# A mixer's triangular solve laid out one 16x16 block a partition, its row loads and decays grouped, a full-width matmul, and an output norm on a chain of its own

## The chip, the cores and the metric

The kernel runs on one core of one Trainium2 chip. The metric is the device time of one execution in microseconds (us), as the median of several runs. A core has five engines that run side by side, each through its own queue of instructions in order: TensorE (PE; its weight loads are shown as PEld), VectorE (DVE), ScalarE (ACT), GpSimd (POOL) and SyncE (SP). SyncE computes nothing here; it issues every transfer between the chip's memory and the core's on-chip memory (SBUF). TensorE writes into PSUM, eight banks of accumulators. On-chip memory has 128 partitions.

## The reference

One decoder layer over 256 tokens of width 2048, in float32: a SwiGLU feed-forward block, a token mixer, a second feed-forward block, and a last norm. Each of the three blocks is preceded by a norm that is shifted and scaled by a conditioning vector, and its result is gated by that vector. The change lies in the mixer:

```python
proj = h @ w_in                      # q, k, v of both head groups, gates, z
# heads 0..7 "fox": softmax attention with a decay given by summed log-sigmoid gates, then a norm
# heads 0..7 "gdn": gated delta rule over chunks of 64 tokens
decay = exp(where(incl, g[..., :, None] - g[..., None, :], -inf))
lower = where(strict, einsum("bhnid,bhnjd->bhnij", kb, k) * decay, 0.0)
t_inv = triangular_solve(eye + lower, eye)          # 64 x 64, unit lower triangular
u = t_inv @ vb;  w = t_inv @ (kb * exp(g))
a_intra = where(incl, einsum("bhnid,bhnjd->bhnij", q, k) * decay, 0.0)
# for each chunk: v_new = u - w @ state;  o = (q * exp(g)) @ state + a @ v_new;  state is updated
o_g = rmsnorm(o_g) * silu(z)
return concatenate([o_f, o_g]) @ w_out
```

So each gdn head needs, for each of its four chunks, the inverse of a 64 x 64 unit lower triangular matrix, and then a chain through four chunks.

## The kernel before

**Weights.** All weight matrices are cut into tiles of 128 x 128 and packed in the order of use. `Stream.next` loads eight tiles at a time (512 KB, `wraw`, L92), ScalarE rounds the block (`whi`, L95) and VectorE takes the rest (`wlo`, L98), so that products of two or three passes reach float32 accuracy. Three buffers of each kind let loads run ahead. Between the blocks the modulation columns are computed at a rate given by `RATE`: a load of 1 MB (`adat`, L212) and a product with a sum on VectorE (L214).

**Order of the work.** The program is written out by Python loops. Projections of the mixer are written by `project` (weights stationary, L613 to L615) and `project_rows` (activations stationary, L626 to L628). After each weight tile `tick` adds 0.35 us to a counter, and when a chain's due time has come, the next piece of that chain is written at this place: a chain is a Python generator, and `yield 1.4` says that its next piece is due 1.4 us later (times a factor `GAP`). Each kind of chain ("k" for keys and solve, "gdn", "fox") runs its members one after the other. `finish` writes what is left of a chain at once. The build then orders each engine's queue starting from this order and its own estimate of what is ready, and sets all waits; the queue's order on the chip is fixed, so an instruction that waits holds all behind it on its engine. `tc.issue_after(x)` keeps an instruction behind x in its queue.

**The sequence.** `ORDER` is a list of steps: K (keys of one gdn head), G (its queries and values), F (a fox head), Z and V (gates z and fox values of four heads). The first projection takes the gates and K0 to K2 together. Then follow K3 to K7, Z0, G0, V0, F0, G1 and so on, and last the out projection of 256 tiles, four output columns first.

**Gates, keys, solve.** `gates` computes running sums of the gates, writes them as rows to DRAM (`rows`, L700) and keeps columns in `colS`. `keys(h)` loads a head's row, broadcast to all partitions (`row_of`, L712), makes the decay from it (`decay(h, 0)`, L723 and L725), and leaves `Ln[:, h]` = -beta k k^T decay (L770). After four heads `solve` inverts the 16 x 16 diagonal blocks of these four heads' two tiles of 128 x 128: 8 tiles with 8 blocks each. It stores the blocks to DRAM (`ld`, eight transfers, L783) and reads them back so that each of a block's 16 partitions holds the whole block (eight broadcast reads of 128 KB, L788), into columns of `x`, which the mixer uses as spare room: `x` itself is kept in `xd` in DRAM meanwhile and comes back by `x_back` (L600). Then 15 steps of a product (L795) and a sum (L796) on VectorE substitute, and L798 spreads the result into `U0`. `gdn(h)` starts with `U0` (L818, L820) and doubles the block size twice, 16 to 32 to 64.

**The chunk loop** of `gdn` (L899 to L921): `wq` holds, per tile, the four slots of 64 columns w, q, q, w. One matmul (L908) gives both w times state and q times state in two halves of a PSUM bank; L909 makes the new values in `vz`, whose other half is zero; L911 adds a times the new values to the half that holds q times state; L915 gives the state's update. Then `orw` is normed and gated (L924 to L933), and after `yield 7.0` it is transposed (L938) and split for the out projection.

**The end.** After the last step all chains are finished, `x_back` is called for all four quarters, and the out projection runs over its operands in the order `ko`: gdn 0 to 3, fox 0 to 7, gdn 4 to 7.

Of the kernel before, what the change touches and what calls it, by code (L numbers as in the profile page):

```python
# [16 lines left out]
P = 128  # L17
# [24 lines left out]
GAP = {"k": 1.0, "gdn": 1.0, "fox": 1.2}  # L42
ORDER = ("K3 K4 K5 K6 K7 Z0 G0 V0 F0 G1 F1 G2 F2 G3 F3 V1 Z1 G4 F4 G5 F5 G6 F6 G7 F7").split()
# [6 lines left out]
for _k, _w in (  # L50
    ("foxm", 384), ("mL", 128), ("mU", 128), ("zm", 2 * 64), ("blk", 4), ("id16", 16),
    ("tri", 128), ("tri64", 128), ("tru64", 128), ("sgn", GR),
):
    CST[_k] = (_n, _w)
    _n += _w
# [54 lines left out]
def layer_kernel(ctx: ExitStack, tc: tile.TileContext, xt, c, adaw, cols, cst, w, out, order, dbg=None):  # L110
# [222 lines left out]
    chains = {"k": [], "gdn": [], "fox": []}  # L333
    due = {"k": 0.0, "gdn": 0.0, "fox": 0.0}
# [240 lines left out]
    def mixer():  # L575
# [5 lines left out]
        ld = dram("ld", [2 * NH, 8, 16, 16])  # L581
# [61 lines left out]
        def gates(ps):  # L643
# [61 lines left out]
            V.tensor_scalar(ng, colS[:, :, 1], -1.0, None, ALU.mult)  # L705
            yield 1.0

        def row_of(h, kind, tag):

            rb = m2p.tile([P, T], F32, name="rw", tag="rw" + tag)  # L710
            with tc.issue_after(W.last):
                nc.sync.dma_start(rb, rows[h : h + 1, kind * T : (kind + 1) * T].broadcast_to([P, T]))  # L712
            return rb
# [4 lines left out]
        def decay(h, up):  # L718

            gb = row_of(h, 1, "g")  # L720
            gbv = gb.rearrange("p (t j) -> p t j", t=2)
            dd = m2p.tile([P, 2, P], F32, name="dec", tag=f"dec{up}")
            V.tensor_tensor(dd, bc(C("mU" if up else "mL")), gbv, ALU.add if up else ALU.subtract)  # L723
            for t in range(2):
                A.activation(dd[:, t], dd[:, t], AF.Exp, bias=ng[:, t, h : h + 1] if up else colS[:, t, 1, h : h + 1])  # L725
            if up:
                A.activation(gb, gb, AF.Exp)
            return dd, gb

# [17 lines left out]
        def keys(h):  # L747
# [3 lines left out]
            dec, _ = decay(h, 0)  # L751
            yield 1.0
# [16 lines left out]
            for t in range(2):  # L769
                V.scalar_tensor_tensor(Ln[:, h, t], pg[:, t * P : (t + 1) * P], nb2[:, t : t + 1], dec[:, t], ALU.mult, ALU.mult)  # L770

        def solve(half):
# [7 lines left out]
            Lh = Ln[:, hs4].rearrange("p h t j -> p (h t) j")  # L780
            for b in range(8):
                r = slice(16 * b, 16 * b + 16)
                nc.sync.dma_start(ld[ht, b].rearrange("n r c -> r n c"), Lh[r, :, r])  # L783
            rows_ = x[:, ht]
            for b in range(8):
                r = slice(16 * b, 16 * b + 16)
                src = ld[ht, b].rearrange("n r c -> n (r c)").unsqueeze(0).to_broadcast([16, n, 256])
                nc.sync.dma_start(rows_[r], src)  # L788
            yield 9.0
            U = tmp.tile([P, n, 16], F32, name="u16", bufs=1)  # L790
            pr = tmp.tile([P, n, 16], F32, name="pr16", bufs=1)
            G.memset(rows_[:, :, 0:256:17], 1.0)
            V.tensor_copy(U, C("id16").unsqueeze(1).to_broadcast([P, n, 16]))
            for i in range(1, 16):
                V.tensor_tensor(pr[:, :, : i + 1], rows_[:, :, 16 * i : 16 * i + i + 1], U[:, :, : i + 1], ALU.mult)  # L795
                V.tensor_reduce(U[:, :, i], pr[:, :, : i + 1], mybir.AxisListType.X, ALU.add)  # L796
            for q in range(2):
# [3 lines left out]
                    C("blk").unsqueeze(1).unsqueeze(3).to_broadcast([P, 4, 4, 16]), ALU.mult)  # L801
            yield 1.0
# [3 lines left out]
        def gdn(h):  # L806
# [59 lines left out]
            V.tensor_tensor(wq[:, :, 1:3, :], q_[:, 0].rearrange("p (t c i) -> p t c i", t=2, c=2),  # L866
# [25 lines left out]
            V.tensor_copy(wq[:, :, 0:4:3, :], pu[:, T:].rearrange("p (t c i) -> p t c i", t=2, c=2))  # L892
# [5 lines left out]
            for c_ in range(4):  # L898
# [7 lines left out]
                else:  # L906
                    new = vz[:, c_ - 1]
                    PE.matmul(pc_, wq[:, t, 2 * ev : 2 * ev + 2].rearrange("p a i -> p (a i)"), st, start=True, stop=True)  # L908
                    V.tensor_sub(new[r], u[r, t], pc_[r])  # L909
# [290 lines left out]
```

## Time and profile before

| what | value |
|---|---|
| time, median of 3 runs | 2102.22 us (2100.92 to 2103.65) |
| the profiled execution's own time | 2100.31 us |
| its span, first to last instruction | 2098.5 us |
| TensorE busy | 2041.5 us (97%) |
| VectorE busy | 1565.8 us (75%) |
| ScalarE busy | 1013.5 us (48%) |
| mean TensorE clock granted | 0.982 |
| read from HBM | 514.74 MB |

In the lists of the profile a group of instructions is shown as line, engine, operation, output <- inputs, shapes, xcount, then busy us, the mean ns of one, and idle time of the engine before them with what ended it. A list of waits reads: who waited <- for whom: us in total, times, longest. SPq and DVEq are the engines' queues. A timeline gives start, length, engine, line, operation and names. A list of transfers gives count, KB each, and the median us from issue to landing. A stretch's PE clock is the share of full speed that was granted.

### The profile page before, as it was taken

Reading aid. Unit: us, or ns where it says so; the run is one execution under the profiler, and the core shown is the slowest. Engines: PE = TensorE matmul, PEld = TensorE weight load, DVE = VectorE, ACT = ScalarE, POOL = GpSimd, SP = SyncE. Lnnn points to the kernel's source line nnn. Section 1 sums busy time; section 2 is a strip of 40 time slices with the busy share of each in tenths; the row PEclk is TensorE's granted clock in tenths of the full one; section 3 lists DMA queues with packets and bytes.
Section 4 is the critical chain, followed back from the end, with each engine's and each line's share of the span. In section 5 each row is a group of like instructions: output and inputs, shape, how many; then the busy total and the mean of one; then the engine's idle time right before and its main releaser. Section 6 shows DMA issues by size and latency. Waiting matters only on the chain.

```text
span 2098.5 us, 33387 instructions
## 1 busy us (share of the span) xinstructions
PE 2041.5 (97%) x12965; PEld 1828.9 (87%) x12966; DVE 1565.8 (75%) x2394; ACT 1013.5 (48%) x1579; POOL 63.7 (3%) x58
## 2 busy tenths in 40 slices
PE   8999999999999999889999999999999999999997
PEld 6999999888888888779989978788888888888886
DVE  6899878888888988877878878866666555555554
ACT  4544544333444446645656644554443344444442
POOL 0000000000000120000000002000000000000011
PEclk8999999999999999999999999999999999999998
DMA  8989867999888885765666567566766555555553
GB/s 313 349 324 324 278 206 265 358 344 362 331 327 334 326 292 176 209 249 215 229 231 221 212 210 284 206 239 224 240 234 217 188 184 190 184 188 190 185 188 111
DMA packets 129488, 521.26 MB, mean 248 GB/s; under 512 B 16425, under 2 KB 21545, under 8 KB 111153
## 3 DMA queue, kind: packets, MB, share of 16 engines
q1 hardware_dynamic: 129330, 519.13, 70.1%
q8 instruction: 102, 1.67, 0.3%
q14 instruction: 56, 0.46, 0.1%
HBM read 514.74 MB, written 4.34 MB: 247 GB/s over the span
## 4 chain that ended last, share of the span: by engine, by line
PE 90%; DVE 5%; DMA 2%; ACT 1%; issue 1%; SPq 0%; DVEq 0%; ACTq 0%; POOL 0%; POOLq 0%
PE pd L361 15%; PE pu L361 11%; PE pg L361 11%; PE pd L362 8%; PE pg L362 5%; PE pu L362 5%; PE pgu L431 5%; PE pgu L429 5%; PE pgu L430 5%; PE pp L613 3%; PE pp L614 3%; PE pp L615 3%; PE po L361 3%; DVE wlo L98 2%; PE po L362 1%; DMA wraw<-in_w_dram 1%
## 5 line engine op out<-in xcount | busy, mean ns | idle before, releaser
L98 DVE TENSOR_TENSOR wlo<-wraw,whi 128x1024 fp32r<-128x1024 f32 x674 | 824.2, 1229 | 347.7 <-ACT whi L95 344.4
L95 ACT CAST whi<-wraw 128x1024 fp32r<-128x1024 f32 x674 | 701.4, 1047 | 681.8 <-issue 172.3
L361 PE MATMUL pd<-hid,whi 128*128 128x512 f32 x1408 | 497.2, 397 | 0.0
L362 PE MATMUL pd<-hid,wlo 128*128 128x256 f32 x1408 | 396.1, 282 | 0.8 <-DVE wlo L98 0.7
L361 PE MATMUL pg<-hs,whi 128*128 128x512 f32 x960 | 342.1, 397 | 2.3 <-DVE hs L304 1.8
L361 PE MATMUL pu<-hs,whi 128*128 128x512 f32 x960 | 342.9, 398 | 0.0
L214 DVE CUSTOM_DVE_ANT_0 adat<-adat,cs,colt 128x2048 f32<-128x2048 f32 x140 | 329.2, 2352 | 14.2 <-DMA adat<-in_ada_dram 13.8
L361 PEld LDWEIGHTS pd<-hid,whi 128*128 128x128 f32 x1408 | 264.2, 188 | 64.8
L362 PE MATMUL pg<-hs,wlo 128*128 128x256 f32 x960 | 270.4, 282 | 0.0
L362 PE MATMUL pu<-hs,wlo 128*128 128x256 f32 x960 | 269.9, 281 | 0.0
L362 PEld LDWEIGHTS pd<-hid,wlo 128*128 128x128 f32 x1408 | 265.5, 189 | 2.5 <-DVE wlo L98 2.1
L429 PE MATMUL pgu<-hs,whi 128*128 128x256 f32 x896 | 251.2, 283 | 4.6 <-ACT hs L300 3.8
L431 PE MATMUL pgu<-hs,wlo 128*128 128x256 f32 x896 | 250.8, 284 | 2.4 <-DVE wlo L98 2.3
L430 PE MATMUL pgu<-hs,whi 128*128 128x256 f32 x896 | 252.4, 283 | 0.0
L361 PEld LDWEIGHTS pg<-hs,whi 128*128 128x128 f32 x960 | 180.7, 188 | 45.7 <-issue 2.1
L361 PEld LDWEIGHTS pu<-hs,whi 128*128 128x128 f32 x960 | 180.7, 188 | 43.9
L613 PE MATMUL pp<-hs,whi 128*128 128x256 f32 x656 | 192.8, 295 | 6.7 <-ACT whi L95 5.3
L615 PE MATMUL pp<-hs,wlo 128*128 128x256 f32 x656 | 188.4, 288 | 1.6 <-DVE wlo L98 1.6
L614 PE MATMUL pp<-hs,whi 128*128 128x256 f32 x656 | 188.6, 287 | 0.0
L362 PEld LDWEIGHTS pg<-hs,wlo 128*128 128x128 f32 x960 | 181.7, 189 | 0.0
L362 PEld LDWEIGHTS pu<-hs,wlo 128*128 128x128 f32 x960 | 181.6, 189 | 0.0
L429 PEld LDWEIGHTS pgu<-hs,whi 128*128 128x128 f32 x896 | 170.8, 191 | 6.0 <-ACT hs L300 4.2
(306 smaller groups left out, 2436.6 us busy)
## 6 DMA issues: line engine op xcount, KB each, us to landing
wraw<-in_w_dram SPq DMA_DIRECT2D x674, 512.0 KB, 4.2
adat<-in_ada_dram SPq DMA_DIRECT2D x140, 1024.0 KB, 6.6
rw<-rowd SPq DMA_DIRECT2D x24, 128.0 KB, 6.6
x<-in_x_dram SPq DMA_DIRECT2D x4, 512.0 KB, 5.8
adaf<-in_ada_dram SPq DMA_DIRECT2D x4, 512.0 KB, 8.0
adaf<-in_ada_dram SPq DMA_DIRECT2D x2, 1024.0 KB, 11.8
xd<-x SPq DMA_DIRECT2D x4, 512.0 KB, 6.4
x<-ld SPq DMA_DIRECT2D x16, 128.0 KB, 6.1
```

Source lines behind the costliest of these rows:

```text
L95: nc.scalar.copy(self.h, r)
L98: nc.vector.tensor_tensor(self.l, r, self.h.bitcast(F32), ALU.subtract)
L214: V.tensor_tensor_reduce(t, t, cs, 1.0, L("adab", q, 1), ALU.mult, ALU.add, mod[:, q : q + 1])
L361: PE.matmul(ps, wt[0], act.rearrange("p a t -> p (a t)"), start=first, stop=False)
L362: PE.matmul(ps[:, :T], wt[1], act[:, 0], start=False, stop=last)
L429: PE.matmul(o, wh, hs[:, k, 0], start=first and s == 0, stop=False, skip_group_check=skip)
L430: PE.matmul(o, wh, hs[:, k, 1], start=False, stop=False, skip_group_check=skip)
L431: PE.matmul(o, wl, hs[:, k, 0], start=False, stop=last, skip_group_check=skip)
L613: PE.matmul(pp[i][:, :T], wh, hs[:, k, 0], start=(k == 0), stop=False)
L614: PE.matmul(pp[i][:, :T], wh, hs[:, k, 1], start=False, stop=False)
L615: PE.matmul(pp[i][:, :T], wl, hs[:, k, 0], start=False, stop=(k == KD - 1))
```

## The change

The blocks of `L` now go to one partition each: 64 partitions hold 64 blocks of 16 x 16. The eight stores to DRAM stay, two at a time with yields between them; one read brings the 64 blocks back; the substitution runs with products of i x i elements in step i (rows of the inverse kept transposed); the result is stored (`lt`), and read back in the layout of `U` in pieces of 16 numbers. Every one of these transfers is kept behind the weight load written last.

The keys' decays are made for four heads at once, in `Ln` itself: one transfer (`fetch_rows`) brings four rows to `x`'s columns, one subtraction and eight exponentials make them (`decays`), and `keys` multiplies in place. The second half's rows are fetched after the first half's solve. `decay(h)` is left for queries only, and its row, like the fox heads' rows, is now requested before the head's projection.

In the chunk loop `wq` holds q, w, w, q, so that L908's q half lies where the chunk's own rows lie, and L911 uses all 128 columns of `At` and writes the whole bank. The output's transposes become a chain "out" of their own. G7 is put before F6. The chains are no longer finished before the out projection: they go on between its tiles, each is finished where its operand is first used, and `x_back` is called before the first group's last operand. `V1` first finishes the "k" chain.

```diff
-GAP = {"k": 1.0, "gdn": 1.0, "fox": 1.2}
-ORDER = ("K3 K4 K5 K6 K7 Z0 G0 V0 F0 G1 F1 G2 F2 G3 F3 V1 Z1 G4 F4 G5 F5 G6 F6 G7 F7").split()
+GAP = {"k": 1.0, "gdn": 1.0, "fox": 1.2, "out": 1.0}
+ORDER = ("K3 K4 K5 K6 K7 Z0 G0 V0 F0 G1 F1 G2 F2 G3 F3 V1 Z1 G4 F4 G5 F5 G6 G7 F6 F7").split()
...
-        ld = dram("ld", [2 * NH, 8, 16, 16])
+        ld = dram("ld", [2 * NH, 8, 256])
+        lt = dram("lt", [2 * NH, 8, 256])
...
+            yield 2.0
+            fetch_rows(0)
             yield 1.0
 
         def row_of(h, kind, tag):
 
-            rb = m2p.tile([P, T], F32, name="rw", tag="rw" + tag)
+            rb = m2p.tile([P, T], F32, name="rw", tag="rw" + tag, bufs=3 if tag == "g" else 2)
...
-        def decay(h, up):
-
-            gb = row_of(h, 1, "g")
+        def decay(h):
+
+            gb = rowg.pop(h)
...
+        def fetch_rows(half):
+
+            rowk[half] = x[:, 4 * half : 4 * half + 4]
+            src = rows[4 * half : 4 * half + 4, T:]
+            with tc.issue_after(W.last):
+                nc.sync.dma_start(rowk[half], src.unsqueeze(0).to_broadcast([P, 4, T]))
+
+        def decays(half):
+
+            hs4 = slice(4 * half, 4 * half + 4)
+            yield 5.0
+            rv = rowk[half].rearrange("p h (t j) -> p (h t) j", t=2)
+            mL = C("mL").unsqueeze(1).to_broadcast([P, 8, P])
+            V.tensor_tensor(Ln[:, hs4].rearrange("p h t j -> p (h t) j"), mL, rv, ALU.subtract)
+            for h in range(4 * half, 4 * half + 4):
+                for t in range(2):
+                    A.activation(Ln[:, h, t], Ln[:, h, t], AF.Exp, bias=colS[:, t, 1, h : h + 1])
+            yield 1.0
...
-            dec, _ = decay(h, 0)
-            yield 1.0
...
-                V.scalar_tensor_tensor(Ln[:, h, t], pg[:, t * P : (t + 1) * P], nb2[:, t : t + 1], dec[:, t], ALU.mult, ALU.mult)
+                V.scalar_tensor_tensor(Ln[:, h, t], pg[:, t * P : (t + 1) * P], nb2[:, t : t + 1], Ln[:, h, t], ALU.mult, ALU.mult)
...
+            yield 1.5
             for b in range(8):
                 r = slice(16 * b, 16 * b + 16)
-                nc.sync.dma_start(ld[ht, b].rearrange("n r c -> r n c"), Lh[r, :, r])
-            rows_ = x[:, ht]
-            for b in range(8):
-                r = slice(16 * b, 16 * b + 16)
-                src = ld[ht, b].rearrange("n r c -> n (r c)").unsqueeze(0).to_broadcast([16, n, 256])
-                nc.sync.dma_start(rows_[r], src)
-            yield 9.0
-            U = tmp.tile([P, n, 16], F32, name="u16", bufs=1)
-            pr = tmp.tile([P, n, 16], F32, name="pr16", bufs=1)
-            G.memset(rows_[:, :, 0:256:17], 1.0)
-            V.tensor_copy(U, C("id16").unsqueeze(1).to_broadcast([P, n, 16]))
+                with tc.issue_after(W.last):
+                    nc.sync.dma_start(ld[ht, b].rearrange("n (r c) -> r n c", r=16), Lh[r, :, r])
+                if b % 2:
+                    yield 1.4
+            yield 2.0
+            B = slice(0, 8 * n)
+            blk, xt_, pr = (x[B, j] for j in range(4, 7))
+            with tc.issue_after(W.last):
+                nc.sync.dma_start(blk, ld[ht].rearrange("n b e -> (n b) e"))
+            yield 6.0
+            G.memset(xt_, 0.0)
+            G.memset(xt_[:, 0:256:17], 1.0)
+            bv, xv, pv = (t_.rearrange("p (i j) -> p i j", i=16) for t_ in (blk, xt_, pr))
             for i in range(1, 16):
-                V.tensor_tensor(pr[:, :, : i + 1], rows_[:, :, 16 * i : 16 * i + i + 1], U[:, :, : i + 1], ALU.mult)
-                V.tensor_reduce(U[:, :, i], pr[:, :, : i + 1], mybir.AxisListType.X, ALU.add)
+                V.tensor_tensor(pv[:, :i, :i], xv[:, :i, :i], bv[:, i, :i].unsqueeze(1).to_broadcast([8 * n, i, i]), ALU.mult)
+                V.tensor_reduce(xv[:, :i, i], pv[:, :i, :i], mybir.AxisListType.X, ALU.add)
+            yield 5.0
+            with tc.issue_after(W.last):
+                nc.sync.dma_start(lt[ht].rearrange("n b e -> (n b) e"), xt_)
+            yield 3.0
+            U = x[:, 7, :P].rearrange("p (n i) -> p n i", n=n)
+            with tc.issue_after(W.last):
+                nc.sync.dma_start(U, lt[ht].rearrange("n b (q i) -> (b q) n i", q=16))
+            yield 5.0
...
+            if half == 0:
+                fetch_rows(1)
             yield 1.0
...
-            V.tensor_tensor(wq[:, :, 1:3, :], q_[:, 0].rearrange("p (t c i) -> p t c i", t=2, c=2),
+            V.tensor_tensor(wq[:, :, 0:4:3, :], q_[:, 0].rearrange("p (t c i) -> p t c i", t=2, c=2),
...
-            V.tensor_copy(wq[:, :, 0:4:3, :], pu[:, T:].rearrange("p (t c i) -> p t c i", t=2, c=2))
+            V.tensor_copy(wq[:, :, 1:3, :], pu[:, T:].rearrange("p (t c i) -> p t c i", t=2, c=2))
...
-                    V.tensor_sub(new[r], u[r, t], pc_[r])
+                    V.tensor_sub(new[r], u[r, t], pc_[ro])
                     yield 1.2
-                PE.matmul(pc_[ro], At[:, t, 64 * ev : 64 * ev + 64], new, start=(c_ == 0), stop=True,
-                          skip_group_check=True)
+                PE.matmul(pc_, At[:, t], new, start=(c_ == 0), stop=True, skip_group_check=True)
...
-            A.copy(orw[:64], pov[64:, :, 0])
-            A.copy(orw[64:], pov[:64, :, 1])
+            A.copy(orw[:64], pov[:64, :, 0])
+            A.copy(orw[64:], pov[64:, :, 1])
...
-            yield 7.0
+            start("out", h, to_out(h, orw))
+            yield 0.2
+
+        def to_out(h, orw):
+            yield 6.0
             pt_ = pss("pot")
...
-            cb = row_of(h, 0, "f")
+            cb = rowf.pop(h)
...
+            if h % 4 == 0:
+                start("k", h, decays(h // 4))
             start("k", h, keys(h))
...
+                rowg[h] = row_of(h, 1, "g")
...
+                finish("out", h - 3)
...
-                ups[h] = decay(h, 1)
+                ups[h] = decay(h)
...
+                if h:
+                    finish("k", NH)
                 pv = project_rows("vf", h)
...
+                rowf[h] = row_of(h, 0, "f")
...
-        for kind in chains:
-            finish(kind, NH)
-        for q in range(4):
-            x_back(q)
-
-
-        ko = [NH + h for h in range(4)] + list(range(NH)) + [NH + h for h in range(4, NH)]
+
+
+        ko = [NH + h for h in range(4)] + list(range(6)) + [NH + h for h in range(4, NH)] + [6, 7]
...
             for i, k in enumerate(ko):
+                for kind in ("gdn", "out") if k >= NH else ("fox",):
+                    finish(kind, k % NH)
+                if js[0] == 0 and i == KD - 1:
+                    for q in range(4):
+                        x_back(q)
                 for q, j in enumerate(js):
                     mm(pj[q], W.next("o", k, j), oh_[k], i == 0, i == KD - 1)
+                    tick(TILE_US)
```

More of the change, by code (lines that the diff above doesn't have):

```diff
@@ L50 @@
 for _k, _w in (
-    ("foxm", 384), ("mL", 128), ("mU", 128), ("zm", 2 * 64), ("blk", 4), ("id16", 16),
+    ("foxm", 384), ("mL", 128), ("mU", 128), ("zm", 2 * 64), ("blk", 4),
     ("tri", 128), ("tri64", 128), ("tru64", 128), ("sgn", GR),
@@ L332, in layer_kernel @@
     clock = {"now": 0.0}
-    chains = {"k": [], "gdn": [], "fox": []}
-    due = {"k": 0.0, "gdn": 0.0, "fox": 0.0}
+    chains = {"k": [], "gdn": [], "fox": [], "out": []}
+    due = {k: 0.0 for k in chains}
     def advance(kind):
@@ L716, in mixer @@
         bh = lambda c_, n: c_.unsqueeze(1).to_broadcast([n, 2, 64])
-        def decay(h, up):
-            gb = row_of(h, 1, "g")
+        def decay(h):
+            gb = rowg.pop(h)
             gbv = gb.rearrange("p (t j) -> p t j", t=2)
-            dd = m2p.tile([P, 2, P], F32, name="dec", tag=f"dec{up}")
-            V.tensor_tensor(dd, bc(C("mU" if up else "mL")), gbv, ALU.add if up else ALU.subtract)
+            dd = m2p.tile([P, 2, P], F32, name="dec")
+            V.tensor_tensor(dd, bc(C("mU")), gbv, ALU.add)
             for t in range(2):
-                A.activation(dd[:, t], dd[:, t], AF.Exp, bias=ng[:, t, h : h + 1] if up else colS[:, t, 1, h : h + 1])
-            if up:
-                A.activation(gb, gb, AF.Exp)
+                A.activation(dd[:, t], dd[:, t], AF.Exp, bias=ng[:, t, h : h + 1])
+            A.activation(gb, gb, AF.Exp)
             return dd, gb
+        rowg, rowf, rowk = {}, {}, {}
+        def fetch_rows(half):
[13 more added lines that the diff above has]
+            yield 1.0
         Tms = [m1p.tile([P, 2, P], F32, name=f"Tm{i}") for i in range(2)]
@@ L1108, in constants @@
     put("blk", ic // 16 == np.arange(4)[None, :])
-    put("id16", i % 16 == np.arange(16)[None, :])
     put("tri", i <= j)
```

## The prediction

> **What bounds the kernel now.** I read the page first, then 10 us windows, then TensorE's waits, then SyncE's own timeline.
>
> ```profile
> span 2098.5 us, 33387 instructions
> PE 2041.5 (97%) x12965; PEld 1828.9 (87%) x12966; DVE 1565.8 (75%) x2394; ACT 1013.5 (48%) x1579; POOL 63.7 (3%) x58
> ```
>
> TensorE sets the time, so a change pays only where TensorE stands, runs at a lower clock, or does something dearly. The mixer runs from about 794 to 1331 us. Two places in it stand out.
>
> ```profile
> 860.00:920.00 60.00, 45.36 (x237) 38.60 (x236) 46.80 (x135) 28.18 (x57) 0.62 (x2) 0.83 0.78 212
> 1230.00:1250.00 20.00, 14.85 (x72) 11.37 (x71) 11.10 (x36) 7.59 (x18) 0.00 (x0) 0.74 0.43 134
> 860.00:870.00 10.00, 8.58 (x49) 7.04 (x47) 8.07 (x32) 6.32 (x26) 0.00 (x0) 1.00 0.82 110
> ```
>
> Columns: stretch, length, busy PE, PEld, DVE, ACT, POOL, then PE clock, DMA share, GB/s. From 860 to 920 PE is idle 60 - 45.36 = 14.6 us, and the clock averages 0.83, so 0.17 x 60 = 10.2 us of clock is missing. Clock missing while PE stands costs nothing more; I count 6 of the 10.2 as falling on work (two waits, below, lie partly in the slow time). Lost there: about 21 us. From 1230 to 1250 it is 5.15 idle and 0.26 x 20 = 5.2 of clock, again about half on work: about 8 us.
>
> ```profile
> PE pv L626 <- ACT whi L95: 5.9, 1, 5.9
> PE pp L613 <- ACT whi L95: 5.3, 1, 5.3
> PE pp L615 <- DVE wlo L98: 1.6, 1, 1.6
> ```
>
> In the first place PE waits for weights. SyncE's timeline (start, length, line, count) says why:
>
> ```profile
> 850.47 1.82 SPq L92 DMA_DIRECT2D wraw<-in_w_dram  x2
> 852.34 0.42 SPq L212 DMA_DIRECT2D adat<-in_ada_dram  x1
> 853.33 1.08 SPq L712 DMA_DIRECT2D rw<-rowd  x2
> 857.15 4.14 SPq L783 DMA_DIRECT2D ld<-Ln  x8
> 861.33 3.75 SPq L788 DMA_DIRECT2D x<-ld  x8
> 865.48 0.34 SPq L712 DMA_DIRECT2D rw<-rowd  x1
> 866.20 1.32 SPq L92 DMA_DIRECT2D wraw<-in_w_dram  x2
> ```
>
> No weight block is issued from 852.3 to 866.2, 13.9 us, because solve's sixteen transfers and the row loads stand in the queue. Behind them the eight broadcast reads move 1 MB at 110 GB/s with the DMA engines 82% busy (window 860 to 870). The cover can be read here: a hold of 13.9 us cost PE a 5.9 us wait, so about 7 to 8 us without a weight issue is hidden. The second half does the same:
>
> ```profile
> 879.33 3.89 SPq L783 DMA_DIRECT2D ld<-Ln  x8
> 883.32 3.69 SPq L788 DMA_DIRECT2D x<-ld  x8
> 887.10 11.68 SPq L92 DMA_DIRECT2D wraw<-in_w_dram  x4
> ```
>
> The second place is the end of the mixer: head 7's chain has no projection left to hide under, and the out projection waits for its last operands.
>
> **Part 1: solve and rows.** Per half the change keeps the eight stores, replaces the eight broadcast reads with one read of 64 KB, and adds a store and a read of 64 KB after the substitution.
>
> ```profile
> rw<-rowd SPq DMA_DIRECT2D x24, 128.0 KB, 6.6
> x<-ld SPq DMA_DIRECT2D x16, 128.0 KB, 6.1
> ld<-Ln SPq DMA_DIRECT2D x16, 8.0 KB, 2.7
> ```
>
> (Last number: us from issue to landing.) Issues per half: 16 become 11, and not in one row: the stores go two at a time between weight blocks. The eight row loads for the keys become two of 512 KB. The broadcast megabyte goes. Three dependencies are new: the read waits for the stores (2.7 us by the row above), the last read waits for the store before it (at most 6.1, the row of a larger transfer), and that store waits for VectorE. All but the last lie under the 7 us of cover, so I cost them at nothing; if the cover is gone each costs its own length. The other moved DMAs (a gdn head's row load and a fox head's, now ahead of their projections) pass weight blocks in the queue with one issue each, 0.34 to 0.54 us; nothing is late behind them.
>
> How a read in 64-byte pieces goes is not in the trace. The stores, 128 pieces of 64 bytes, land in 2.7 us; the eight reads, 1024 pieces of 1 KB, occupied the DMA for about 8 us. The read of U has 1024 pieces of 64 bytes, so its cost lies between these; I take 3 us, nearer the stores because the pieces have their size. The Trainium skill (DMA: Bandwidth & Descriptors, Specifications) asks for at least 512 bytes a transfer and says that below it the engine does read-modify-write. If by that rule U's read were as dear as the reads that it replaces, half 0 would keep 8 us and the sum would give 2080 (a rival, below); the stores of 64 bytes here show no such price.
>
> VectorE's work in the stretch, and how it moves:
>
> ```profile
> L795 DVE TENSOR_TENSOR pr<-x,u 128x16 f32<-128x16 f32 (+14 forms) x30 | 7.0, 232 | 4.5 <-DMA wraw<-in_w_dram 2.5 <-POOL x L792 1.4
> L796 DVE TENSOR_REDUCE u<-pr 128x8 f32<-128x16 f32 (+14 forms) x30 | 6.8, 227 | 0.7
> L770 DVE SCALAR_TENSOR_TENSOR Ln<-pkk,nb,dec 128x128 f32<-128x128 f32 x16 | 5.0, 346 | 0.2
> 850.00:911.80 61.80, 47.93 (x262) 41.57 (x261) 49.95 (x155) 31.59 (x69) 0.62 (x2) 0.83 0.78 211
> 911.80:966.00 54.20, 53.43 (x348) 46.92 (x347) 41.53 (x73) 32.00 (x61) 0.00 (x0) 1.00 0.65 238
> ```
>
> The substitution is (7.0 + 6.8)/2 = 6.9 us a half. In the new layout instruction i has i x i elements a partition in place of 8(i+1): 1240 against 1080 in all.
>
> ```profile
> 872.44 0.17 DVE L795 TENSOR_TENSOR pr<-x,u 128x16 f32<-128x16 f32 x1 [1.36 <-POOL x L792]
> 888.33 0.29 DVE L795 TENSOR_TENSOR pr<-x,u 128x128 f32<-128x128 f32 x1
> ```
>
> 112 more elements cost 0.12 us, 1.1 ns each, so 160 more, in two instructions, cost 0.35 us a half: nothing. These rows also show that 6.9 us of work took 16 us, because weights (L98), modulation (L214) and the other half's keys stood between.
>
> Going by the yields and 0.35 us a weight tile, the old program writes the second half's substitution 76 us after the mixer's first matmul, inside G0. The new one writes it at 110 us, in F0, after keys 4 to 7 at 87 to 93 us; U0 of half 0 comes at 77, before head 0 wants it at 87. So about 6.9 + 0.8 + 2.5 + 1.3 = 11.5 us of VectorE work (substitution, U0, half of L770, its small companions) leaves a stretch where VectorE was busy 49.95 of 61.8 us, and lands in one with 54.2 - 41.5 = 12.7 us free. Nearly all of that stretch's slack is then used, and wlo, which PE waits for, is on the same engine. **I give back 4 us for it, and 2 us for head 0 arriving at U0 early**; between nothing and all 21 regained I take 15.
>
> **Part 2: At at full width.** The attention matmul of the state loop (L911) used 64 columns; it becomes 128. Rows: start, length.
>
> ```profile
> 984.22 0.28 PE L615 MATMUL pp<-hs,wlo 128*128 128x256 f32 x1
> 984.34 0.38 PE L908 MATMUL po<-st,wq 128*128 128x128 f32 x2
> 984.47 0.36 PE L613 MATMUL pp<-hs,whi 128*128 128x256 f32 x1
> 984.67 0.28 PE L614 MATMUL pp<-hs,whi 128*128 128x256 f32 x1
> ```
>
> From L615 to L614 is 0.45 us with two wide matmuls of 0.12 in it, so the two passes of the 128-column L908 cost 0.21.
>
> ```profile
> 995.35 0.28 PE L615 MATMUL pp<-hs,wlo 128*128 128x256 f32 x1
> 995.56 0.43 PE L911 MATMUL po<-vz,At 128*64 128x128 f32 x2
> 995.92 0.39 PE L613 MATMUL pp<-hs,whi 128*128 128x256 f32 x1
> 996.15 0.28 PE L614 MATMUL pp<-hs,whi 128*128 128x256 f32 x1
> ```
>
> Here the same sum is 0.80 - 0.24 = 0.56: the narrow pair costs 0.34 more. There are 8 heads x 4 = 32 of them: 10.9 us, on the engine that bounds, in stretches where PE is busy throughout. The nearest row for the new form is L908: same bank, same shape. From below the gain is nothing (the price is of something else, or VectorE then bounds); I take 9.5, since VectorE, 41.5 of 54.2 us busy in the stretch quoted and fuller with the moved work, may hold back a little. The swapped halves of wq only rename rows; the copies and the subtraction keep their shapes and cost the same.
>
> **Part 3: the end.** The out norm's transposes become a chain of their own, so head h+1 starts 7 us of yields earlier; G7 goes before F6; the closing steps are written between the out projection's tiles instead of before them. By the yields, head 7's output is then ready 9 us after F7 and first used 18 us after it. So the 8 us should go. Against that x_back, 2 MB, moves to the end of the first group.
>
> ```profile
> 1219.60:1261.00 41.40, 36.25 (x204) 30.15 (x204) 25.75 (x66) 17.26 (x37) 0.00 (x0) 0.88 0.63 220
> SPq L600 <- DVE orw L933: 9.5, 1, 9.5
> x<-xd SPq DMA_DIRECT2D x4, 512.0 KB, 4.5
> ```
>
> Today SyncE stands 9.5 us at x_back for head 7, weights behind it, while PE stands anyway. Moved, it no longer waits, but PE no longer stands either: its price is between nothing (512 KB land in 4.5 us, and 7 us are covered) and 6 us (2 MB at 220/0.63 = 349 GB/s, this stretch's rate with the DMA engines full). I take 2: gain 6. One pool of three PSUM banks now serves the out chain and the next head together: nothing, because the transposes come 6 us apart, and up to 2 us in all if each head waits 0.3.
>
> **The sum.** 15 + 9.5 + 6 = 30.5 us. The profiled execution took 2100.3 us (span 2098.5 and 1.8 around it), 1.9 under the median of the runs. 2100.3 - 30.5 = 2069.8, on the median's footing 2071.7: **2071 us**.
>
> **Rivals.**
> - **Head 0 stands at U0** (16%). The new route to U0 has three DMA round trips and a substitution that took 16 us for 6.9 of work; PE takes its queue in order. For it: by the yields there are only 10 us between U0 and its use. Against it: DMA is freed there. One wait like today's 5.9, with 3 of clock, would take 9 of the 15: 2081. The Trainium skill (TensorE: Matmul & The Clock Gate, Why this matters for your kernels) puts the loss of the clock at gaps above some 3 us; by that a wait under 3 costs only itself, 2075 at most; the two waits above, both longer, do show the low clock.
> - **U's small pieces are dear** (4%): its 1024 pieces occupy the DMA engines as the 1024 of the old reads did, 8 us in which weights wait; half 1's lie far from any use. 2080. Against it: the 2.7 us of the stores.
> - **The narrow price stays or VectorE takes it** (12%): no 9.5, so 2081. For it: VectorE's fill in the stretches after 911. Against: L908 beside it.
> - **x_back takes what the end gains** (8%): 6 us of weights late in place of 2, so 2076.
> - **Slower: SyncE is held by the new dependent transfers** (7%). Seven waits (read, store, read in each half, and the second row load behind U0) each hold the queue longer than the 7 us covered. The second hold today (879.3 to 887.1) cost PE 5.3 us, 1.6 for a late wlo, and some 2.7 of clock, 9.6; seven make 67, against 40 gained: 2129. It decides from five of the seven. For it: VectorE needed 16 us where the yields leave 6. Against: SyncE's waits for such results are short today, since the queue's order puts weights ahead:
>
> ```profile
> SPq L783 <- DVE pr L795: 1.8, 1, 1.8
> ```
>
> - **The parts cancel** (5%): the four before the slower one together give back 9 + 8 + 9.5 + 4 = 30.5, so 2102.
>
> **How the numbers follow.** Forecast 48%, its own range 2062 (all 40 us regained) to 2078; rivals in their order 16, 4, 12, 8, 7 and 5%. The range 2058 to 2090 leaves out the slower case and the cancelled one; below 2062 it allows for small waits elsewhere in the mixer. A measurement of this kernel tells about 0.2%, 4.2 us, from no change: faster 0.88 (48 + 16 + 4 + 12 + 8), same 0.05, slower 0.07.
>
> **What would show it.** In the new profile: no weight gap over 8 us on SyncE between 850 and 920 us, and no slow clock there (Part 1); L911's successors at the same spacing as L908's, 0.21 us a pair (Part 2); no PE wait for orw and a first out group of about 64 x 0.35 = 22 us plus chain work, where it took 41 (Part 3). It is wrong if PE waits for U0 in pu0 or for wlo for over 6 us in V0 to G1, if weights wait behind lt or x_back, or if the second PE gap only moves.

## The result: a third less than forecast

The changed kernel takes **2081.4 us** (median of 4 runs, 2078.4 to 2086.5) where the kernel before, in the same session, takes 2102.0 (2100.9 to 2103.7): a ratio of 0.9905, 95% interval 0.9893 to 0.9918. That is 20.6 us less; 30.5 were forecast, with 2071 us as the time. The page's first lines:

```profile
span 2076.6 us, 33353 instructions
PE 2029.3 (98%) x12965; PEld 1825.4 (88%) x12966; DVE 1559.8 (75%) x2386; ACT 1012.5 (49%) x1577; POOL 66.8 (3%) x60
```

The span fell by 21.9 us (the profiled execution was the shortest of its four). To see where, I cut both traces where the last projection matmul of each step (for the out groups, the last of each group) starts. The rows below are, in order, Z0, G0, all from V0 to F7, the first group of the out projection (four columns, 64 tiles), and its second (one column, 16 tiles). Columns as in the prediction: length, busy PE, PEld, DVE, ACT, POOL, clock, DMA share, GB/s. Before:

```profile
854.38:889.84 35.46, 28.43 (x122) 22.62 (x121) 29.81 (x100) 18.61 (x46) 0.31 (x1) 0.86 0.81 200
889.84:911.72 21.88, 15.04 (x104) 14.49 (x103) 15.81 (x45) 8.53 (x12) 0.31 (x1) 0.77 0.76 234
911.72:1219.55 307.83, 306.94 (x2233) 282.55 (x2232) 247.51 (x543) 189.43 (x394) 0.00 (x0) 1.00 0.62 223
1219.55:1261.12 41.57, 36.42 (x206) 30.27 (x204) 25.92 (x66) 17.26 (x37) 0.00 (x0) 0.88 0.64 221
1261.12:1267.34 6.22, 5.83 (x33) 4.83 (x32) 6.22 (x10) 3.56 (x6) 3.94 (x3) 1.00 0.72 267
```

After:

```profile
855.50:879.31 23.81, 22.96 (x104) 18.42 (x103) 20.16 (x56) 12.02 (x25) 0.00 (x0) 1.00 0.68 242
879.31:893.53 14.22, 12.46 (x97) 11.79 (x96) 11.86 (x20) 11.19 (x14) 0.00 (x0) 1.00 0.74 242
893.53:1209.29 315.76, 311.50 (x2312) 292.22 (x2310) 262.04 (x625) 194.94 (x423) 0.43 (x2) 1.00 0.64 224
1209.29:1234.88 25.59, 25.43 (x151) 21.92 (x150) 18.66 (x46) 12.56 (x27) 0.00 (x0) 1.00 0.78 284
1234.88:1243.70 8.82, 6.42 (x33) 4.89 (x32) 6.51 (x11) 4.98 (x8) 5.18 (x3) 1.00 0.49 192
```

| stretch | before | after | difference |
|---|---|---|---|
| Z0 and G0 | 57.3 | 38.0 | -19.3 |
| V0 to F7 | 307.8 | 315.8 | +7.9 |
| out, first group | 41.6 | 25.6 | -16.0 |
| out, second group | 6.2 | 8.8 | +2.6 |

Both bad places are gone: the clock is 1.00 in all five rows, where it was 0.86, 0.77 and 0.88. But PE's idle time between V0 and F7 went from 0.9 us (307.83 - 306.94) to 4.3, 79 more matmuls lie there, and the second out group now has 2.4 us of idle time. The time before Z0 (1.1 us more) and after the second out group (1.7 more) make up the rest of the difference in span.

### The profile page after: what moved, and what is told of

The parts are those of the page before. It is cut to its first block, busy times and chain, and to the rows that moved or that the text cites. A ratio compares the mean times of both kernels' runs of the same rounds, so it can differ in the third digit from the quotient of the medians.

```text
span 2076.6 us, 33353 instructions
## 1 busy us (share of the span) xinstructions
PE 2029.3 (98%) x12965; PEld 1825.4 (88%) x12966; DVE 1559.8 (75%) x2386; ACT 1012.5 (49%) x1577; POOL 66.8 (3%) x60
## 4 chain that ended last, share of the span: by engine, by line
PE 87%; DVE 6%; DMA 2%; ACT 2%; issue 1%; DVEq 0%; SPq 0%; ACTq 0%
PE pd L361 15%; PE pu L361 11%; PE pg L361 11%; PE pd L362 8%; PE pg L362 5%; PE pu L362 5%; PE pgu L431 5%; PE pgu L429 5%; PE pgu L430 5%; PE po L361 3%; PE pp L614 2%; PE pp L616 2%; PE pp L615 2%; DVE wlo L98 2%; PE po L362 1%
## 5 line engine op out<-in xcount | busy, mean ns | idle before, releaser
L214 DVE CUSTOM_DVE_ANT_0 adat<-adat,cs,colt 128x2048 f32<-128x2048 f32 x140 | 329.3, 2352 | 16.5 <-DMA adat<-in_ada_dram 16.1
```

The source lines that it names most:

```text
L214: V.tensor_tensor_reduce(t, t, cs, 1.0, L("adab", q, 1), ALU.mult, ALU.add, mod[:, q : q + 1])
```

## What the signs say that the prediction named

SyncE's timeline of the changed kernel (start, length, line, count), around the first half's stores:

```profile
852.52 0.33 SPq L92 DMA_DIRECT2D wraw<-in_w_dram  x1
852.90 0.43 SPq L212 DMA_DIRECT2D adat<-in_ada_dram  x1
858.15 4.66 SPq L806 DMA_DIRECT2D ld<-Ln  x8
862.91 0.86 SPq L92 DMA_DIRECT2D wraw<-in_w_dram  x2
863.99 0.52 SPq L813 DMA_DIRECT2D x<-ld  x1
```

Between 850 and 920 there is one gap without a weight block over 8 us, from 852.9 to 862.9: the eight stores were issued together after all, in spite of the yields between them. PE lost little by it: it was idle for 23.81 - 22.96 = 0.85 us in all of Z0. So here 10 us without a weight load were nearly covered, where the prediction read 7 to 8. It isn't a fixed number: before the change the second hold left 10.0 us without a weight load too (877.1 to 887.1), and PE stood 5.3 us for it. The difference may be that weights were already late there from the first hold; no run tests it. No wait of PE for U0 exists. One sign of being wrong did come true: weights wait behind `x_back`, and PE stands 2.4 us for them in the second out group (see the run with the loads apart). The reads of the new route land in about 5 us, where the prediction took 3 for U's (count, KB, us from issue to landing):

```profile
x<-ld SPq DMA_DIRECT2D x2, 64.0 KB, 4.8
x<-lt SPq DMA_DIRECT2D x2, 64.0 KB, 5.4
```

U's read (`x<-lt`) in 1024 pieces of 64 bytes takes 5.4 us, the read of as many bytes in 64 pieces of 1 KB 4.8. The Trainium skill (DMA: Bandwidth & Descriptors, Specifications) asks for 512 bytes or more in a transfer for the full rate. At this size the trace shows 0.6 us more for the smaller pieces (medians of two reads each, at different times), not the 8 us by which the prediction's rival priced it.

For the full-width matmul, two places of PE's timeline (start, modelled length). Before, a narrow pair L911 with the state's update L915 behind it:

```profile
982.24 0.28 PE L614 MATMUL pp<-hs,whi 128*128 128x256 f32 x1
982.45 0.43 PE L911 MATMUL po<-uz,At 128*64 128x128 f32 x2
982.81 0.49 PE L915 MATMUL pst<-uz,kbd 128*128 128x128 f32 x2
983.06 0.36 PE L615 MATMUL pp<-hs,wlo 128*128 128x256 f32 x1
983.26 0.28 PE L613 MATMUL pp<-hs,whi 128*128 128x256 f32 x1
```

After, such two pairs (L945, L948) where nothing stands between:

```profile
972.48 0.28 PE L615 MATMUL pp<-hs,whi 128*128 128x256 f32 x1
972.60 0.38 PE L945 MATMUL po<-vz,At 128*128 128x128 f32 x2
972.82 0.39 PE L948 MATMUL pst<-vz,kbd 128*128 128x128 f32 x2
972.96 0.36 PE L616 MATMUL pp<-hs,wlo 128*128 128x256 f32 x1
973.16 0.28 PE L614 MATMUL pp<-hs,whi 128*128 128x256 f32 x1
```

With 0.12 taken off for each of the two wide matmuls, as in the prediction, the two pairs cost 1.02 - 0.24 = 0.78 us before and 0.68 - 0.24 = 0.44 after: the full 0.34. Where two such pairs stand alone between projection matmuls (worked out from the starts in the traces), the median went from 0.78 at 19 places to 0.49 at 20 (the expectation below took 0.53). Half of the 20 lie at 0.44 to 0.46; at the others, up to 0.74, a pair starts late.

## The experiments

Each time stands against the kernel before, run beside it; "gain" is the difference of the medians.

### One part at a time

**At alone**: the kernel before with only this.

```diff
-            V.tensor_tensor(wq[:, :, 1:3, :], ...q...)
+            V.tensor_tensor(wq[:, :, 0:4:3, :], ...q...)
...
-                PE.matmul(pc_[ro], At[:, t, 64 * ev : 64 * ev + 64], new, ...)
+                PE.matmul(pc_, At[:, t], new, start=(c_ == 0), stop=True, skip_group_check=True)
...  (the other half of wq, the subtraction and the copies of orw follow)
```

> The kernel before with Part 2 alone: L911 at 128 columns, the halves of wq swapped. Theory of the prediction: a narrow pair costs 0.34 us more than a wide one, 32 pairs, so 9.5 to 10.9 us, about 2092. From the changed kernel's trace, where the wide pair with its successor still takes 0.53 us in place of 0.44, I would now say 7 to 9: 2093 to 2095. Rival (the price is not the width's, or VectorE takes it): within 4 us of 2102.

Measured: 2098.6 us, ratio 0.9988 (0.9978 to 0.9997), a gain of 2.2.

**The end alone**: the chain "out", G7 before F6, closing steps between the out projection's tiles, `x_back` in the first group.

```diff
...
+            start("out", h, to_out(h, orw))
...
-        for kind in chains:
-            finish(kind, NH)
-        for q in range(4):
-            x_back(q)
...
+                if js[0] == 0 and i == KD - 1:
+                    for q in range(4):
+                        x_back(q)
```

> The kernel before with Part 3 alone: the out chain, G7 before F6, the closing steps between the out projection's tiles, x_back before the last operand. Prediction: 6 us, 2096. Rival (x_back takes what the end gains): 2100 to 2102, with PE waiting for whi or wlo behind x_back in the second group of the out projection for more than 5 us. In the changed kernel that wait is 2.4 us in all, so I lean to 2097.

Measured: 2097.7, ratio 0.9984 (0.9975 to 0.9994), a gain of 3.1.

**Solve and rows alone**: the changed kernel with the other two parts undone.

> The changed kernel without Parts 2 and 3, that is, the kernel before with the new solve, the grouped decays and the row loads ahead. Prediction: 15 us, 2087. If the three parts simply add (21 us in all, 8 for Part 2, 5 for Part 3), 8 us: 2094. If the clean stretch of the changed kernel (Z0 and G0 take 38.0 us there, 57.3 before) holds here too and nothing is given back later, 18: 2084.

Measured: 2089.6, ratio 0.9946 (0.9929 to 0.9963), a gain of 11.2.

**The changed kernel with the narrow At** (the first diff reversed).

> The changed kernel with L911 narrow again, Parts 1 and 3 kept. If Part 2 is worth the same here as alone, the time is that of the changed kernel plus the gain of Part 2 alone: 2081 + 8 = 2089 (prediction's size: 2091). If VectorE bounds the stretches after G0 in the changed kernel, where more of its work lies, the narrow price is partly hidden: 2082 to 2085.

Measured: 2086.7, ratio 0.993 (0.9915 to 0.9944), a gain of 14.1, so that At is worth about 6 us there (20.6 - 14.1 = 6.5 by the gains, 2086.7 - 2081.4 = 5.3 by the times), where alone it was worth 2.2. In its trace the stretch from G0's end to F7's end is 7.7 us longer than the changed kernel's, and all of that is PE's busy time (319.3 against 311.5). The second out group is 2.7 us longer there as well (11.5 against 8.8), where no narrow matmul runs, so the 5 to 6 us aren't purely At's. The three solo gains add to 16.5, the whole gives 20.6: the parts seem to help each other. The rows from G0's end to F7's end say how. At alone, then the end alone (with its second out group), then both in the kernel before:

```profile
912.24:1217.93 305.69, 300.72 (x2234) 283.09 (x2232) 246.45 (x538) 189.11 (x394) 0.00 (x0) 1.00 0.63 224
```

```profile
911.52:1227.10 315.58, 314.53 (x2286) 288.87 (x2284) 251.12 (x558) 192.20 (x403) 0.00 (x0) 1.00 0.62 220
1253.57:1263.91 10.34, 7.92 (x34) 6.16 (x32) 7.11 (x11) 4.42 (x7) 5.17 (x3) 0.83 0.53 211
```

```profile
911.47:1220.72 309.25, 308.08 (x2285) 289.35 (x2284) 249.66 (x558) 194.35 (x405) 0.00 (x0) 1.00 0.63 225
```

**At and the end together**, without the new solve:

> The kernel before with Part 2 (At at full width) and Part 3 (the end), without the new solve. Alone the two gave 2.2 and 3.1 us. If their gains are independent, together they give 5.3: some 2095. If Part 2's saving was eaten in the kernel before because G0 to F7 waits on each head's chain, and the out norm as a chain of its own starts the next head earlier and so takes these waits away, the two together give 9 to 12: 2089 to 2092. If they get in each other's way, under 4: over 2097.

Measured: 2091.6, ratio 0.995 (0.9936 to 0.9965), a gain of 9.2, which is more than 2.2 + 3.1 and at the lower edge of the second theory. At alone takes 6.2 us of busy time from PE (306.94 to 300.72), but PE's idle time rises from 0.9 to 5.0 us. My reading is that PE, which takes its queue in order, now reaches a matmul before VectorE or ScalarE has its operand, and that the narrow pairs' extra time had covered that. Its waits there are short, the longest two by the list of waits (the first is for a weight block's low part, the second for an operand of a gdn chain):

```profile
PE pp L615 <- DVE wlo L98: 1.3, 1, 1.3
PE pn L860 <- DVE Z L837: 1.1, 1, 1.1
```

With the out norm on a chain of its own the same saving (314.53 to 308.08, 6.5) leaves PE's idle time as it is (1.05 and 1.17), and the stretch is 6.3 us shorter. So Part 2's gain hangs on Part 3; which of Part 3's edits does it was not separated. And 9.2 + 11.2 = 20.4: these two groups add up to the whole.

### The solve: queue or megabyte

**The old solve, its transfers written two at a time between weight blocks.**

```diff
-                nc.sync.dma_start(ld[ht, b].rearrange("n r c -> r n c"), Lh[r, :, r])
+                with tc.issue_after(W.last):
+                    nc.sync.dma_start(ld[ht, b].rearrange("n r c -> r n c"), Lh[r, :, r])
+                if b % 2:
+                    yield 1.4
...  (the eight reads likewise)
-            yield 9.0
+            yield 5.0
```

> The kernel before with solve's own transfers spread: the eight stores and the eight broadcast reads of 128 KB are kept, but go two at a time between weight blocks, with 1.4 us between the pairs. If the loss in the first stretch came from SyncE standing at sixteen transfers in a row, most of what the new solve gains alone (11 us) comes back: 2091 to 2094. If it came from the broadcast megabyte, which keeps the DMA engines full for 8 us at 110 GB/s, the weights stay late: 2098 to 2102.

Measured: 2115.1, ratio 1.0073 (1.0058 to 1.0088): 15 us slower. Z0 and G0 take 33.09 + 13.41 = 46.5 us, 10.8 less than before, but V0 goes from 29.9 to 54.9:

```profile
904.05:958.92 54.87, 39.02 (x156) 30.34 (x155) 33.03 (x82) 18.52 (x36) 0.31 (x1) 0.75 0.49 155
```

On SyncE the transfers of the first half still went out in one row, eight stores and eight reads, with no weight block between 859.9 and 870.8:

```profile
860.33 5.63 SPq L784 DMA_DIRECT2D ld<-Ln  x8
866.00 3.75 SPq L792 DMA_DIRECT2D x<-ld  x8
```

Of the second half's only the reads were parted, four and four. The edit did delay the work: the second half's substitution moved into V0, where head 0's chain wants VectorE and ScalarE (PE waits 4.0 us for a transpose's operand behind a product of the substitution, 3.7 for `At`; ScalarE 8.9 for PE). So this edit didn't spread the transfers as it was meant to, and the run doesn't tell the queue from the megabyte.

**The old solve with short reads**: all sixteen transfers stay, each read brings one row of a block, 8 KB for 128 KB. The rest of each block is zero, so what is inverted is not L.

```diff
+            if h in (0, 1):
+                G.memset(x[:, 8 * h : 8 * h + 8], 0.0)
...
-                src = ld[ht, b].rearrange("n r c -> n (r c)").unsqueeze(0).to_broadcast([16, n, 256])
-                nc.sync.dma_start(rows_[r], src)
+                src = ld[ht, b, 0].unsqueeze(0).to_broadcast([16, n, 16])
+                nc.sync.dma_start(rows_[r, :, :16], src)
```

> The kernel before, whose eight broadcast reads a half read only the first row of each block (8 KB a transfer where it was 128 KB; the rest of the blocks is set to zero by GpSimd once, so the inverse computed is not that of L). The number of transfers and their place in SyncE's queue stay. If the loss between Z0 and the end of G0 (57 us, of which 38 after the change) comes from SyncE's queue being held, as the prediction's reading of the cover has it, Z0 and G0 stay at 55 to 58 us and the time within 2 us of before. If it comes from the megabyte that the reads move while weights want the same DMA engines, Z0 and G0 fall by 8 us or more and the time by about as much. Between the two, 3 to 7 us, both have a share.

Measured: 2095.0, ratio 0.9969 (0.9958 to 0.998), a gain of 5.8.

```profile
855.45:887.35 31.90, 27.01 (x122) 21.64 (x121) 27.40 (x97) 18.75 (x46) 0.31 (x1) 0.89 0.55 166
887.35:907.26 19.91, 15.25 (x103) 14.52 (x102) 17.09 (x49) 9.08 (x12) 0.32 (x1) 0.83 0.70 245
```

Z0 and G0 take 51.8 us, 5.5 less. PE still waits there for weights behind the sixteen short transfers, 4.1 and 2.9 us where it was 5.9 and 5.3:

```profile
PE pv L626 <- ACT whi L95: 4.1, 1, 4.1
PE pp L613 <- ACT whi L95: 2.9, 1, 2.9
```

So of the 19.3 us that the change regains there, some 5.5 belong to the megabyte, and the queue has a share too. How large it is isn't shown: of the other 14 us a part is matmuls that the change moves out of Z0 and G0 (24 fewer in the changed kernel's two rows than in these).

**The changed kernel with the rows requested late**, as before, when they are wanted.

```diff
-                rowg[h] = row_of(h, 1, "g")
...
-            gb = rowg.pop(h)
+            gb = row_of(h, 1, "g")
...  (the fox heads' rows likewise)
```

> The changed kernel with the row loads of the query decays and of the fox heads requested where the kernel before requested them, when they are wanted, and not before the head's projections. The prediction costed the earlier request at nothing: then the time is within 2 us of the changed kernel's 2081 (a gain of 18 to 22 us against the kernel before). If the earlier rows hide a wait of ScalarE or VectorE for a row in every step, 16 steps with some 0.5 us each: 8 us longer, 2089. If the earlier rows stand in front of weights, it is faster than 2079.

Measured: 2085.5, ratio 0.9923 (0.9906 to 0.994), a gain of 15.3: about 5 us less than with early rows, though the intervals overlap. G0 and V0, first with late rows, then the changed kernel's V0 (its G0 stands above):

```profile
879.77:891.39 11.62, 11.62 (x98) 11.58 (x96) 10.71 (x21) 4.83 (x7) 0.00 (x0) 1.00 0.80 270
891.39:931.76 40.37, 34.52 (x172) 28.01 (x171) 29.87 (x81) 26.89 (x62) 0.42 (x2) 0.92 0.59 197
```

```profile
893.53:924.51 30.98, 29.90 (x162) 24.28 (x161) 26.73 (x62) 21.17 (x48) 0.43 (x2) 1.00 0.66 244
```

Together 52.0 against 45.2 us. It is not 16 steps with a little each, but one place: with late rows PE waits in V0 2.9 us for head 0's `qv` and 1.6 at a keys' product, behind VectorE's `At`. The rest of the run partly evens it out: from F0 to F7 it is 2.3 us shorter, and its second out group is 2.7 us longer. The prediction's nothing for this edit was probably too little; how a late row makes `qv` late was not followed further.

### The end, and who holds the later chains

**x_back's four loads apart**, in the changed kernel.

```diff
-                if js[0] == 0 and i == KD - 1:
-                    for q in range(4):
-                        x_back(q)
+                for q in range(4):
+                    if (js[0], i) == ((0, KD - 3), (0, KD - 1), (4, 6), (7, 6))[q]:
+                        x_back(q)
```

> The changed kernel with x_back's four loads apart: the first two before the 14th and the last operand of the first group, the third in the group of column 4, the fourth in that of column 7. If x_back's 2 MB in one row make the weights late (the second group takes 8.8 us there, 10.3 and 11.5 in the two variants beside it, against 5.65 of matmuls), the time falls by 3 us or a little more: 2077 to 2079. If the lateness has another cause (VectorE's eight residual steps, 3.1 us, before three weight blocks), nothing changes: 2081.

Measured: **2076.2** (2074.0 to 2078.2), ratio 0.9885 (0.987 to 0.99), a gain of 23.8, the best of all. The second out group is back at 6.2 us (worked out as in the table). ScalarE's wait for a weight block says why; the changed kernel, then this one:

```profile
ACT whi L95 <- DMA wraw<-in_w_dram: 5.7, 2, 5.5
```

```profile
ACT whi L95 <- DMA wraw<-in_w_dram: 4.1, 2, 2.6
```

With the four loads in a row the DMA engines are full from 1226 to 1234 us, ScalarE stands 5.5 us for a weight block, and PE's waits in the changed kernel's second group follow it (with the loads apart they aren't there):

```profile
PE po L361 <- ACT whi L95: 1.6, 2, 1.2
PE po L362 <- DVE wlo L98: 0.8, 1, 0.8
```

The interval of this run and the changed kernel's (0.9893 to 0.9918) overlap a little, so that the 3 us between them rest on the traces too. And the price of four loads in a row isn't fixed: the second group takes 8.8 us in the changed kernel, 10.3 and 10.4 in the two runs with the end but without the new solve, 11.5 with the narrow At and with late rows, but 6.3 in the next two runs below. In the first of these the third group is 1.6 us longer instead; in the second the first group is 33.5 us long and gives the loads time.

**VectorE relieved**: the modulation columns are moved out of the stretch after G0.

```diff
-(280, 0.25), (408, 0.125)
+(280, 0.1), (330, 0.6), (346, 0.28), (408, 0.125)
```

> The changed kernel with the modulation columns moved in time, their number kept: 0.1 a weight block in place of 0.25 in the fifty blocks from Z0's first to F3's last, 0.6 in V1 and Z1, 0.28 after. It takes some 7 of 12 columns, 2.35 us each on VectorE, 17 us in all, out of the stretch into which the second half's solve moved. If VectorE's load costs PE time there (the 4 us given back in the prediction), the time falls by 3 to 5: 2076 to 2078. If the waits there are of latency and not of load, under 2 us of difference: 2080 to 2083.

Measured: 2081.0, ratio 0.9903 (0.9887 to 0.992): as the changed kernel. Six of the twelve columns left the stretch from Z0 to F3, and it got no shorter, so VectorE's mean load isn't what holds the chains there.

**The steps of a head's chain 1.35 times as far apart.**

```diff
-GAP = {"k": 1.0, "gdn": 1.0, "fox": 1.2, "out": 1.0}
+GAP = {"k": 1.0, "gdn": 1.35, "fox": 1.2, "out": 1.0}
```

> The changed kernel with the factor on the gdn chain's yields at 1.35 in place of 1.0, so that its steps are written further apart; the out chain leaves 7 us a head for it. In Part 2 alone 5.9 us of matmul time went and 3.8 us came back as longer time at the next steps of the chains. If these are waits of TensorE for an operand that VectorE or ScalarE has not finished, wider steps take them away: 3 to 8 us, 2073 to 2078. If the time is the matmuls' own, nothing changes or the end gets later: 2081 to 2084.

Measured: 2078.2 (2077.5 to 2079.2), ratio 0.9895 (0.988 to 0.991), a gain of 21.9: not to be told from the changed kernel's 20.6.

**Both of these that looked better**: loads apart and steps wider.

> The changed kernel with x_back's four loads apart and with the steps of a head's chain 1.35 times as far apart. Apart from each other these gave 23.8 and 21.9 us against the kernel before, where the change itself gave 20.6. If the two are independent: 20.6 + 3.2 + 1.3 = 25.1 us, 2076. If wider steps push head 7's chain into the out projection, where x_back's spread loads no longer leave room, 20 to 22 us: 2080.

Measured: 2082.4 (2076.8 to 2083.6), ratio 0.9903 (0.9887 to 0.9918), a gain of 18.4: the second theory, and not to be told from the changed kernel. The trace is of the fastest of its five executions (2076.8; the others took 2081 to 2084), so it doesn't show all of the loss. F7 ends 6.9 us earlier than in the changed kernel (1202.4 against 1209.3), but the first out group takes 36.3 us where it took 25.6: head 7's chain has slid into it, and PE waits 2.6 us for `orw`. What stands is the loads apart alone.

## Why the prediction was too high

The measured 2081 lies in the stated range of 2058 to 2090, but outside the forecast's own 2062 to 2078: all three terms of the sum were too large.

**Part 1, 15 forecast, 11.2 measured alone** (7.8 to 14.9 by its interval). Cause and place were right: weights late behind solve's transfers, of which the short reads give some 5.5 us to the bytes moved and leave the rest to SyncE's hold and to moved work. In the trace of the solve alone the size is near too: 19.4 us come back in Z0 and G0. But what is given back is another thing than VectorE's fill and head 0. V0 to F7, solve alone:

```profile
895.60:1212.16 316.56, 313.48 (x2277) 287.70 (x2276) 260.97 (x615) 195.72 (x421) 0.42 (x2) 1.00 0.64 223
```

PE is busy 6.5 us longer there than before, with 44 more matmuls, and idle 2.2 more. Part of these matmuls had run in Z0 just before PE stood 5.9 us for weights, so that they cost nothing there: without them it would only have stood longer. Keys' products before and with the new solve, in Z0 and G0:

```profile
L757 PE MATMUL pk<-colt,kk x8: 270/272/273, 860.0 to 867.6; 128*128 128x128 f32 x8
L760 PE MATMUL pkk<-kk x16: 274/275/377, 860.2 to 868.7; 128*128 128x128 f32 x16
```

```profile
L778 PE MATMUL pk<-colt,kk x2: 270/270/271, 860.6 to 860.7; 128*128 128x128 f32 x2
L781 PE MATMUL pkk<-kk x4: 274/275/275, 860.8 to 861.1; 128*128 128x128 f32 x4
```

Three quarters of them now run after G0, where they push projections aside at their full length; another part is head 7's, which begins earlier (the first out group is 4.8 us shorter in this run). Z0 also begins 3.3 us later than before, 1.6 of it already at the mixer's first matmul, ahead of the change. Moved PE work appeared in no term of the sum: that is the step that failed here. Nor did the row loads ahead, which the late rows put at some 4 to 5 us of this part, with overlapping intervals.

**Part 2, 9.5 forecast, 2.2 alone and 6.1 beside the end** (9.2 - 3.1). The price of a narrow pair was right as a best case, and it goes with the width; the step that failed is that nearly all of it comes back "in stretches where PE is busy throughout". A busy row says that PE had work, not that the next chain step was ready: PE's idle time took back 4.1 of 6.2 us in At alone and 0.1 of 6.5 beside the end, so the narrow pairs' time was in part cover for VectorE's and ScalarE's steps. The rival that VectorE takes it was right in direction for At alone. Whether through its load was not tested there; in the changed kernel a relieved VectorE changed nothing.

**Part 3, 6 forecast, 3.1 alone.** The gain was sized well: the first out group falls by 15.1 us (41.57 to 26.47), of which 7.75 are head 7's work that now lies before F7's end (315.58 - 307.83): 7.35, where 8 were forecast. Head 7's wait for `orw` is gone from the out projection, and the first group takes 25.6 us in the changed kernel. The mis-sized term is x_back: 2 us taken, 4.1 measured in this part alone (10.34 - 6.22), 2.6 in the changed kernel, 0.1 to 5.3 in the second group of all runs with four loads in a row, which is between its bounds of 0 and 6. The 7 us of cover, read at one place, was used at another where the DMA engines run full; there it didn't hold.

**The rivals.** 2081 was also the time of two of them, but neither is what happened: there is no wait at U0, and the narrow price is gone. The slower case needed PE to wait long for weights behind the new transfers; its longest wait for weights in Z0 and G0 is 0.9 us.

## What to carry to other kernels

An engine that stands still may have done some work for free around the wait; before you claim its idle time, list the instructions beside it and charge them where they will land. An engine with an in-order queue passes a saving on only if the next operand is ready: look for what the removed time was covering, and move the consumers apart (here a second chain) in the same change. A cover read at one place, so many us without a weight load, holds only where the transfers have the same room; here two stretches of 10 us cost 5.3 us in one place and under 1 us in another.

## What the runs showed of the hardware

The clock is lost at shorter waits than the prediction took. In the run with loads apart and wider steps PE stood once for 2.6 us, for `orw`, and once for 1.1, and then ran at half its clock until about 1237.7, some 6 us of work:

```profile
1228.00:1230.00 2.00, 0.00 (x0) 0.00 (x0) 1.86 (x6) 0.00 (x0) 0.00 (x0) 1.00 0.23 94
1230.00:1232.00 2.00, 0.67 (x3) 0.45 (x4) 0.84 (x3) 0.47 (x1) 0.00 (x0) 0.72 0.89 281
1232.00:1234.00 2.00, 2.00 (x7) 1.71 (x8) 0.00 (x0) 0.00 (x0) 0.00 (x0) 0.50 0.78 139
1234.00:1236.00 2.00, 2.00 (x8) 1.71 (x8) 0.34 (x1) 1.04 (x1) 0.00 (x0) 0.50 0.89 326
```

The end alone stood in its second out group for 1.2 and 0.8 us within 2.5 us, and lost the clock too; the changed kernel stood there equally long and kept it:

```profile
1258.00:1260.00 2.00, 2.00 (x8) 1.67 (x7) 1.45 (x2) 0.00 (x0) 2.00 (x1) 0.51 0.82 305
```

```profile
1238.00:1240.00 2.00, 1.45 (x8) 1.32 (x9) 2.00 (x3) 0.81 (x1) 2.00 (x1) 1.00 0.16 63
```

The Trainium skill (TensorE: Matmul & The Clock Gate, Why this matters for your kernels) warns of idle gaps above some 3 us. These rows show that less can do it, and not every time. So a wait of 1 to 3 us, which the prediction's first rival priced at its own length, can cost that and 2 to 3 us of clock behind it. Whether this is why the changed kernel's four runs lie 8 us apart, where nineteen of the kernel before lie 6 apart, was not settled.

Among operands of 128 columns, a pair of float32 matmuls whose stationary operand has 64 columns costs 0.34 us more than a pair with 128 (0.78 - 0.44, above), though it computes half as much. The Trainium skill (TensorEngine Tiling (Array Packing), Key Properties) says that a change of the tiling mode drains TensorE; that fits, but no run here separates the drain from other causes.
